# Column halves of the array for attention's and retention's narrow products in a hybrid decoder layer

## The chip, the cores and the metric

The kernel runs on one NeuronCore of a Trainium2 chip. The core's engines are TensorE (PE: matmul, and PEld for its weight loads), VectorE (DVE), ScalarE (ACT), GpSimd (POOL) and SyncE (SP), each with an instruction queue of its own that it works off in order; DMAs are issued from the queues of SP, ACT and POOL. The metric is the device time of one execution in microseconds, as a median over runs; lower is better.

## The reference

One decoder layer over 256 tokens of width 1024, batch 1, all in fp32:

```python
h = rmsnorm(x, mix_norm_g)
rq, rk, rv, rg, mq, mk, mv, ga, gb = split(h @ w_in)
ret = retention(rotary(rq), rotary(rk) * 64 ** -0.5, rv)        # 8 heads, qk 64, v 128, chunks of 128
y_a = (ret * silu(rg)) @ ret_w_branch
att = moba_attention(head_rmsnorm(mq) * 64 ** -0.5, head_rmsnorm(mk), mv, rel_bias)   # 8 heads of 64
y_b = att @ moba_w_branch
x = x + (sigmoid(ga) * y_a + sigmoid(gb) * y_b) @ w_out
x = x + peer(rmsnorm(x, ffn_norm_g), ...)                        # product-key experts, the larger part
```

With 256 tokens there is a single attention block, so attention is causal softmax attention with a bias per head and distance: `softmax(q k^T + bias) v`. Retention works in chunks of 128 tokens:

```python
scores = (q @ k.T) * decay_in            # within a chunk
o_in = scores @ v
kv = (k * k_decay).T @ v                 # state that a chunk leaves behind: 64 x 128 per head
o_cross = (q @ previous_kv) * q_decay
ret = groupnorm(o_in + o_cross)
```

## The kernel before

The sequence is two tiles (`t`) of 128 tokens. The mixer, about the first 250 us, is one stream of projection pieces. A piece is two blocks of 128 rows of a weight matrix by 512 columns. For each piece `i` the main loop (lines 843 to 852) does, in this order: `load_to` issues ring loads on SP's queue; `cut(i + 3)` splits the weights of a piece three ahead into a high and a low part (ACT writes `rhi`, line 147; DVE subtracts and writes `rlo`, line 148); `products(i)` runs the piece's matmuls on PE (lines 230 to 232 or 239 to 241), twelve of 512 columns in the "nat" mode; `early_turns(i)` turns some expert rows for later (DVE line 751; DMAs on ACT's queue, lines 747 and 763); and `pump()` advances each of the first three open generators by one step, up to its next `yield`. The newest epilogue of a projection stands at the front of that list. So attention and retention are generators whose steps are laced between pieces, and the `yield`s set how many pieces lie between two steps. The order of instructions on each engine is the order in which the Python code issues them; nothing is reordered afterwards.

`attention()` does this for each tile: scores into `side` PSUM tiles (line 361, two heads at a time on the row halves of the array), bias (365), maximum (369), exponent on ACT with the row sums into `ssum` (371), then one over the sums into `rs` on DVE (375). After a `yield` it turns the probabilities on PE (383) and evacuates them as `prT` on ACT (384). Two `yield`s later it multiplies: with `prT` as the stationary operand (128 by 128) and 64 columns of `mv` streaming, so that the result `po` has tokens on the partitions and heads in columns (389). DVE multiplies `po` by `rs` into `at` (393), two `yield`s pass, PE turns `at` (400), and `split_to` cuts the turned result into `ah` and `al` for the next projection (401; ACT at line 147, DVE at line 148).

`retention()` begins with the state `kv`: for each pair of heads one product of all 128 columns of `kdec` with the 256 columns of both heads' `rv` (416), evacuated by ACT (418). The result holds the two useful 64 by 128 blocks and two that nobody reads. Line 428 makes the scores on the row halves, line 441 the products with `rv`, and line 446 adds `q @ kv` for the second chunk.

Buffers: `side()` has four PSUM tiles for all short products; the SBUF tag `t2` has four tiles of 128 by 512, shared by the norms (`qn`), the rotary (`ra`, `rb_`, `rqd`), attention's `at` and the gates. Around attention's first tile the rotary of the retention queries runs: for each tile DVE writes `ra` and `rb_` (320, 322), POOL adds them (324), POOL scales one of them into `rqd` (330), and some pumps later PE turns them (273).

Of the kernel before, what the change touches and what calls it, by code (L numbers as in the profile page):

```python
# [18 lines left out]
AF = mybir.ActivationFunctionType  # L19
OP = mybir.AluOpType  # L20
AX = mybir.AxisListType

P = 128
S = 256
# [3 lines left out]
H = 8  # L28
# [47 lines left out]
def layer_kernel(ctx, tc, x, mix_norm_g, w_in, ret_w_branch, moba_q_gain, moba_k_gain, moba_w_branch,  # L76
# [3 lines left out]
    V, A, G, T = nc.vector, nc.scalar, nc.gpsimd, nc.tensor  # L80
# [16 lines left out]
    def side():  # L97
        return psum.tile([P, 512], F32, name="side", bufs=4)
# [46 lines left out]
    def split_to(hi, lo, src, engine=V):  # L145

        A.activation(hi, src, AF.Copy)
        engine.tensor_tensor(lo, src, hi.bitcast(F32), op=OP.subtract)

    def rsqrt_(pool, a, shape, name):  # L150

        y = pool.tile(shape, F32, name=name + "y", bufs=2)
        m = minus_half if len(shape) == 2 else minus_half.rearrange("p (a b) -> p a b", a=shape[1])
        G.tensor_tensor(y, a, m[:, :shape[1]], op=OP.pow)  # L154
        return y
# [17 lines left out]
    ident = cp.tile([P, P], F32, name="ident")  # L173
# [8 lines left out]
    def t4(shape, name, dt=F32):  # L182
        return wk.tile(shape, dt, name=name, tag="t4", bufs=3)

    def t2(shape, name):
        return wk.tile(shape, F32, name=name, tag="t2", bufs=4)
# [90 lines left out]
    mv = ap.tile([P, NT, 512], F32, name="mv", tag="b4a")  # L277
    rqk = [ap.tile([P, 4, S], F32, name=f"rqk{i}", tag="b4" + "fg"[i]) for i in range(2)]
    rqdT = ap.tile([P, 4, P], F32, name="rqdT")
    kdec = ap.tile([P, 512], F32, name="kdec")  # L280
    rv = [ap.tile([P, D], F32, name=f"rv{i}", tag="b4" + "hi"[i]) for i in range(2)]
    kv = ap.tile([P, 4, S], F32, name="kv", tag="b4c")
# [67 lines left out]
    def attention():  # L350
        ssum = wk.tile([P, NT, H], F32, name="ssum")
        for t in range(NT):
            w = (t + 1) * P
            pr = wk.tile([P, H, S], F32, name="pr")
            nh = 512 // w
            for i0 in range(0, 4, nh):
                ps = [side() for _ in range(2)]
                for j in range(nh):
                    for c in range(2):
                        b = slice(c * 64, (c + 1) * 64)  # L360
                        T.matmul(ps[c][:, j * w:(j + 1) * w], mqk[0][b, i0 + j, t * P:(t + 1) * P],
                                 mqk[1][b, i0 + j, :w], start=True, stop=True)
                for c in range(2):
                    n = slice(4 * c + i0, 4 * c + i0 + nh)
                    V.tensor_tensor(pr[:, n, :w], ps[c].rearrange("p (j k) -> p j k", j=nh),
                                    bias[:, n, S - w:], op=OP.add)
                    yield
            sm = wk.tile([P, H], F32, name="smx")
            V.tensor_reduce(sm, pr[:, :, :w], axis=AX.X, op=OP.max, negate=True)
            for h in range(H):  # L370
                A.activation(pr[:, h, :w], pr[:, h, :w], AF.Exp, bias=sm[:, h:h + 1], accum_out=ssum[:, t, h:h + 1])
                if h % 4 == 3:
                    yield
            rs = wk.tile([P, H], F32, name="rs")
            V.reciprocal(rs, ssum[:, t, :])
            yield
            po = side()
            for kt in range(t + 1):
                prT = t4([P, H, P], "prT")
                for q in range(2):  # L380
                    p = side()
                    for j in range(4):
                        T.transpose(p[:, j * P:(j + 1) * P], pr[:, 4 * q + j, kt * P:(kt + 1) * P], ident)
                    A.activation(prT[:, 4 * q:4 * q + 4, :], p.rearrange("p (j i) -> p j i", j=4), AF.Copy)
                yield
                yield
                for i in range(H):
                    h = 2 * (i % 4) + i // 4
                    T.matmul(po[:, h * 64:(h + 1) * 64], prT[:, i, :], mv[:, kt, h * 64:(h + 1) * 64],
                             start=(kt == 0 and i == 0), stop=(kt == t), skip_group_check=True)  # L390
            at = t2([P, 512], "at")
            for c in range(2):
                V.tensor_tensor(at.rearrange("p (i c d) -> p c i d", c=2, d=64)[:, c],
                                po.rearrange("p (i c d) -> p c i d", c=2, d=64)[:, c],
                                rs[:, 4 * c:4 * c + 4, None].to_broadcast([P, 4, 64]), op=OP.mult)
            yield
            yield
            p = side()
            for c in range(4):
                T.transpose(p[:, c * P:(c + 1) * P], at[:, c * P:(c + 1) * P], ident)  # L400
            split_to(ah[0][:, :, t * P:(t + 1) * P], al[0][:, :, t * P:(t + 1) * P],
                     p.rearrange("p (c q) -> p c q", c=4))
            yield

    def mv_epi(o):
# [3 lines left out]
        yield  # L409

    def retention():
        for q in range(2):
            p = side()
            for j in range(2):
                hp = 2 * q + j
                T.matmul(p[:, j * S:(j + 1) * S], kdec[:, hp * P:(hp + 1) * P], rv[0][:, hp * S:(hp + 1) * S],
                         start=True, stop=True)
            A.activation(kv[:, 2 * q:2 * q + 2, :], p.rearrange("p (j e) -> p j e", j=2), AF.Copy)
            yield
        for t in range(NT):  # L420
            s = slice(t * P, (t + 1) * P)

            st = t4([P, H, P], "st")
            ps = [side() for _ in range(2)]
            for j in range(4):
                for c in range(2):
                    b = slice(c * 64, (c + 1) * 64)
                    T.matmul(ps[c][:, j * P:(j + 1) * P], rqk[1][b, j, s], rqk[0][b, j, s], start=True, stop=True)
            for c in range(2):
                V.tensor_tensor(st[:, 4 * c:4 * c + 4, :], ps[c].rearrange("p (j i) -> p j i", j=4),  # L430
                                decay[:, 4 * c:4 * c + 4, :], op=OP.mult)
                yield
            st6 = wk.tile([P, H, 6], F32, name="st6")
            mvv = wk.tile([P, H, 2], F32, name="mvv")
            va = wk.tile([P, H], F32, name="va")
            nm = wk.tile([P, H], F32, name="nm")
            os_ = [side() for _ in range(2)]
            for c in range(2):
                for j in range(4):
                    h = 2 * j + c  # L440
                    T.matmul(os_[c][:, j * P:(j + 1) * P], st[:, 4 * c + j, :], rv[t][:, h * P:(h + 1) * P],
                             start=(j == 0), stop=(t == 0), skip_group_check=True)
            for j in range(4 if t else 0):
                for c in range(2):
                    b = slice(c * 64, (c + 1) * 64)
                    T.matmul(os_[c][:, j * P:(j + 1) * P], rqdT[b, j, :], kv[b, j, c * P:(c + 1) * P], start=False,
                             stop=True, skip_group_check=True)
            for c in range(2):
                for j in range(4):
                    V.bn_stats(st6[:, 4 * c + j, :], os_[c][:, j * P:(j + 1) * P])  # L450
                yield
            for i in range(H):
                V.bn_aggr(mvv[:, i, :], st6[:, i, :])
            V.tensor_scalar(va, mvv[:, :, 1], EPS, None, op0=OP.add)  # L454
            r = rsqrt_(wk, va, [P, H], "gn")
            yield
            V.scalar_tensor_tensor(nm, mvv[:, :, 0], -1.0, r, op0=OP.mult, op1=OP.mult)
            for c in range(2):
                for j in range(4):
                    h, i = 2 * j + c, 4 * c + j  # L460
                    A.activation(ret[:, t, h * P:(h + 1) * P], os_[c][:, j * P:(j + 1) * P], AF.Identity,
                                 bias=nm[:, i:i + 1], scale=r[:, i:i + 1])
                yield
# [153 lines left out]
    def queries(q):  # L617
# [23 lines left out]
        return epi  # L641

    att, rtn, gtd = attention(), retention(), gated()
    w0 = w_in[0]
    hx = (hh, hl)
# [148 lines left out]
    for t in range(NT):  # L794
        for q in range(2):
            c = slice(512 * q, 512 * (q + 1))
# [3 lines left out]
            p = side()  # L800
# [4 lines left out]
    for q in range(2):  # L805
        for t in range(NT):
            n = slice(t * P, (t + 1) * P)
            A.activation(hh[q][:, :, n], sides[2 * t + q], AF.Copy)
    for q in range(2):
        for t in range(NT):  # L810
            n = slice(t * P, (t + 1) * P)
# [460 lines left out]
    for c in range(NK):  # L1272
# [13 lines left out]
        for k in range(KC):  # L1286
            n = c % 2 * NA
            T.matmul(pa[:, n:n + NA], uT[:, k * P:(k + 1) * P], hT[:, k], start=(c % 2 == 0 and k == 0),  # L1288
                     stop=(k == KC - 1), skip_group_check=True)
# [34 lines left out]
    for c in range(NK):  # L1324
# [14 lines left out]
        if c == NK - 5:  # L1339
# [11 lines left out]
            for b in range(KC):  # L1351
                T.matmul(o[b][:, 2 * ND:2 * ND + NXP], gs["accx"][:, b * P:(b + 1) * P], pick, start=False, stop=True,
                         skip_group_check=True)
# [87 lines left out]
```

## Time and profile before

| what | us |
|---|---|
| median of three runs | 943.9 |
| the three runs | 941.56, 943.9, 944.66 |
| the profiled execution, its own time | 942.91 |
| its span, first to last instruction | 941.1 |
| PE busy | 932.6 |
| DVE busy | 794.2 |
| ACT busy | 521.1 |
| POOL busy | 395.0 |

The time of the profiled execution is its span and 1.8 us around it. Busy times of PE are modelled, since matmuls are pipelined: two rows of PE may overlap, and what a product costs is seen from the start of one to the start of the next. In a row of a timeline stand its start, its length, the engine (with a "q" for its instruction sequencer), the line, and output and inputs by name; "x16" means that sixteen records follow each other. In brackets stand the time that the engine was idle before it and what ended that.

### The profile page before, as it was taken

To read this page: it belongs to the slowest core of one execution; us is meant where nothing else is said; L and a number is where in the kernel's file an instruction comes from. 1 tells how busy PE (TensorE), PEld (TensorE's weight loads), DVE (VectorE), ACT (ScalarE), POOL (GpSimd) and SP (SyncE) were. 2 spreads that over 40 slices of the span, in tenths; PEclk is the share of its full clock that TensorE was granted. 3 is DMA by queue.
4 is the path that set the end of the run, shared out by engine and by line. 5 is a ranking of instruction groups with operands and counts; after the bars stand their busy time and mean duration, and the time that the engine had idled before them with its cause. 6 is when DMAs were issued, how large, how long until landed. Compare 5 with 4: busy or idle time off the path is not lost.

```text
span 941.1 us, 19115 instructions
## 1 busy us (share of the span) xinstructions
PE 932.6 (99%) x7192; PEld 894.4 (95%) x7192; DVE 794.2 (84%) x1518; ACT 521.1 (55%) x953; POOL 395.0 (42%) x305
## 2 busy tenths in 40 slices
PE   8999999999999999999999999999999999999998
PEld 6887898998999999999999999999999999999997
DVE  6658557788678999999998999974979989898977
ACT  6554655544644435444687778776454645454553
POOL 3412010000202447534656667763547556464720
PEclk9999999999999999999999999999999999999999
DMA  9899879998799997999999999999999999999993
GB/s 317 236 236 283 241 207 292 306 295 264 244 354 386 406 400 285 402 402 361 375 401 390 382 364 381 380 377 367 370 363 398 409 383 409 383 409 374 409 344 125
DMA packets 110858, 322.50 MB, mean 343 GB/s; under 512 B 11532, under 2 KB 23701, under 8 KB 110638
## 3 DMA queue, kind: packets, MB, share of 16 engines
q1 hardware_dynamic: 64492, 184.43, 55.0%
q0 software_dynamic: 32512, 115.54, 32.5%
q10 hardware_dynamic: 13762, 21.31, 7.6%
q8 instruction: 57, 0.93, 0.4%
q14 instruction: 35, 0.29, 0.1%
HBM read 308.57 MB, written 14.19 MB: 343 GB/s over the span
## 4 chain that ended last, share of the span: by engine, by line
PE 95%; DMA 2%; DVE 1%; ACT 0%; POOL 0%; issue 0%; SPq 0%; DVEq 0%; ACTq 0%; POOLq 0%
PE acc L1288 24%; PE side L737 11%; PE side L1320 9%; PE acc L1320 9%; PE acc L230 6%; PE acc L231 6%; PE acc L232 6%; PE acc L1321 4%; PE side L1321 4%; PE acc L239 3%; PE acc L240 3%; PE acc L241 3%; DMA raw_ring<-in_peer_v_dram 2%; PE side L1318 1%; PE acc L1318 1%; PE acc L1216 1%
## 5 line engine op out<-in xcount | busy, mean ns | idle before, releaser
L1037 POOL DMA_INDIRECT rows<-in_peer_u_dram,eg x86 | 110.5, 1285 | 68.4 <-DVE rows L1048 30.2
L1037 POOL DMA_INDIRECT rows<-in_peer_v_dram,eg x54 | 96.0, 1777 | 73.2 <-DVE vacc L1123 51.2
L737 PE MATMUL side<-ident,raw_ring 128*128 128x128 f32 x768 | 103.0, 277 | 0.0
L737 PEld LDWEIGHTS side<-ident,raw_ring 128*128 128x128 f32 x768 | 93.0, 192 | 0.0
L1165 ACT ACTIVATE oh_buf<-oh_more,tS 128x128 bf16<-128x128 f16 x176 | 58.4, 417 | 0.5 <-DVE oh_more L1160 0.5
L1123 DVE SCALAR_TENSOR_TENSOR vacc<-rows,av,vacc 128x1024 f32<-128x1024 f32 x43 | 55.1, 1282 | 0.1
L1048 DVE SCALAR_TENSOR_TENSOR rows<-rows,h 128x1024 f32<-128x1024 f32 x43 | 53.2, 1249 | 1.4 <-DMA rows<-in_peer_u_dram,eg 1.4
L1260 ACT ACTIVATE cw<-W 128x352 fp32r<-128x352 f32 x58 | 28.7, 495 | 45.3 <-PE acc L1321 43.9
L1261 DVE TENSOR_TENSOR cw<-W,cw 128x352 fp32r<-128x352 f32 x58 | 30.2, 521 | 19.8 <-ACT cw L1260 19.6
L1246 POOL TENSOR_TENSOR W<-W,gl 128x256 f32<-128x256 f32 (+19 forms) x31 | 26.4, 850 | 41.9 <-ACT gl L1245 34.0
L580 POOL DMA_DIRECT2D x1d<-xt x1 | 0.7, 657 | 88.5 <-DVE xt L562 88.5
L1288 PE MATMUL acc<-hTd,raw_ring 128*128 128x128 f32 x288 | 35.1, 276 | 0.0
L1160 DVE TENSOR_TENSOR oh_more<-iota,tI 128x1024 f16<-128x1024 f16 x44 | 34.3, 780 | 0.0
L1161 DVE TENSOR_TENSOR oh_buf<-oh_more,tM 128x1024 f16<-128x1024 f16 x44 | 32.3, 734 | 2.2
L1288 PEld LDWEIGHTS acc<-hTd,raw_ring 128*128 128x128 f32 x288 | 33.6, 192 | 0.0
L154 POOL TENSOR_TENSOR gny<-va,minus_half 128x8 f32<-128x8 f32 x2 | 4.3, 2126 | 67.8 <-DVE va L454 67.8
L1215 PE MATMUL acc<-oh_buf 128*128 128x128 bf16 x176 | 24.4, 220 | 0.0
L1216 PE MATMUL acc<-oh_buf 128*128 128x128 bf16 x176 | 24.4, 219 | 0.0
L1229 ACT ACTIVATE W<-acc 128x512 f32<-128x512 f32 (+20 forms) x44 | 17.2, 391 | 12.0 <-PE acc L1216 10.6
L1248 ACT ACTIVATE W<-acc 128x256 f32<-128x256 f32 (+19 forms) x52 | 18.5, 356 | 4.4 <-PE acc L1288 4.4
L1231 DVE TENSOR_TENSOR W<-acc,W 128x264 f32<-128x264 f32 (+19 forms) x32 | 16.2, 507 | 4.7 <-ACT W L1229 4.5
L1215 PEld LDWEIGHTS <-oh_buf 128*128 128x128 f16 x176 | 19.8, 114 | 0.0
(2695 smaller groups left out, 3484.4 us busy)
## 6 DMA issues: line engine op xcount, KB each, us to landing
raw_ring<-in_peer_v_dram SPq DMA_DIRECT2D x128, 512.0 KB, 8.2
raw_ring<-in_peer_u_dram SPq DMA_DIRECT2D x96, 512.0 KB, 9.9
raw_ring<-in_w_in_dram SPq DMA_DIRECT2D x52, 512.0 KB, 5.5
raw_ring<-turned SPq DMA_DIRECT2D x18, 512.0 KB, 7.1
raw_ring<-in_peer_w_q_dram SPq DMA_DIRECT2D x16, 512.0 KB, 6.1
W<-in_peer_u_dram SPq DMA_DIRECT2D x14, 512.0 KB, 11.0
eraw<-in_peer_u_dram ACTq DMA_DIRECT2D x36, 128.0 KB, 6.5
h<-in_peer_u_dram ACTq DMA_DIRECT2D x36, 128.0 KB, 6.6
```

Of the source, the lines that this page charges most:

```text
L230: T.matmul(o[t], xh[:, s], wh, start=(k == 0), stop=False)
L231: T.matmul(o[t], xh[:, s], wl, start=False, stop=False)
L232: T.matmul(o[t], xl[:, s], wh, start=False, stop=(k == kc - 1))
L737: T.transpose(p[:, k * P:(k + 1) * P], r.rearrange("p (i k) -> p k i", k=KC)[:, 4 * q + k], ident)
L1037: G.indirect_dma_start(out=r, out_offset=None, in_=tab, in_offset=bass.IndirectOffsetOnAxis(ap=eg[:, j:j + 1], axis=0))
L1048: V.scalar_tensor_tensor(r, r, 1.0, h, op0=OP.mult, op1=OP.mult, accum_out=av[:, j:j + 1])
L1123: V.scalar_tensor_tensor(a, r, av[:, j:j + 1], a, op0=OP.mult, op1=OP.add)
L1165: A.activation(o1[:, j], hot[:, 0, :, j], AF.Copy, scale=tS[:, t, k + j:k + j + 1])
L1215: T.matmul(p[:, j * P:(j + 1) * P], hi, o1, start=True, stop=False)
L1288: T.matmul(pa[:, n:n + NA], uT[:, k * P:(k + 1) * P], hT[:, k], start=(c % 2 == 0 and k == 0), stop=(k == KC - 1), skip_group_check=True)
L1320: T.matmul(o[b][:, :2 * ND], vh[:, n], w, start=(c == 0), stop=False, skip_group_check=True)
L1321: T.matmul(o[b][:, :ND], vl[:, n], w[:, :ND], start=False, stop=(c == NK - 1), skip_group_check=True)
```

## The change

Three things change.

Attention's product with `mv` swaps its operands. The 64 columns of `mv` of one head are now the stationary operand, and the 128 columns of `prT` stream. The result comes out turned: 64 rows (the head's dimensions) by 128 tokens. The two heads of a pair write to partitions 0 to 63 and 64 to 127 of the same PSUM tile, which is to say to the two column halves of the array, one after the other in program order.

Since tokens are now in columns, `rs` can no longer be applied per partition. ACT spreads it to `rr` (128 tokens by 512, each head's value 64 times), directly after the reciprocal. After the last product PE turns `rr` into a new `side` tile, ACT copies that to `at`, and DVE multiplies `at` by `po`. The result is already turned, so the four turns of `at` go away; one `yield` is left before `split_to`, where there were two.

Retention's state uses the column halves too: eight products of 64 columns of `kdec` with 128 columns of `rv`, into one `side` tile, with one evacuation in place of two. `kv` holds only the useful blocks, and line 446 reads them at the new place. The number of `yield`s stays.

```diff
             V.reciprocal(rs, ssum[:, t, :])
+            rr = t2([P, 512], "rr")
+            A.activation(rr.rearrange("p (i c d) -> p i c d", c=2, d=64),
+                         rs.rearrange("p (c i) -> p i c", c=2)[:, :, :, None].to_broadcast([P, 4, 2, 64]), AF.Copy)
             yield
             po = side()
             for kt in range(t + 1):
...
-                for i in range(H):
-                    h = 2 * (i % 4) + i // 4
-                    T.matmul(po[:, h * 64:(h + 1) * 64], prT[:, i, :], mv[:, kt, h * 64:(h + 1) * 64],
-                             start=(kt == 0 and i == 0), stop=(kt == t), skip_group_check=True)
+                for i in range(4):
+                    for c in range(2):
+                        h = 2 * i + c
+                        T.matmul(po[c * 64:(c + 1) * 64, i * P:(i + 1) * P], mv[:, kt, h * 64:(h + 1) * 64],
+                                 prT[:, 4 * c + i, :], start=(kt == 0 and i == 0), stop=(kt == t), skip_group_check=True)
+            p = side()
+            for i in range(4):
+                T.transpose(p[:, i * P:(i + 1) * P], rr[:, i * P:(i + 1) * P], ident)
             at = t2([P, 512], "at")
-            for c in range(2):
-                V.tensor_tensor(at.rearrange("p (i c d) -> p c i d", c=2, d=64)[:, c],
-                                po.rearrange("p (i c d) -> p c i d", c=2, d=64)[:, c],
-                                rs[:, 4 * c:4 * c + 4, None].to_broadcast([P, 4, 64]), op=OP.mult)
-            yield
-            yield
-            p = side()
-            for c in range(4):
-                T.transpose(p[:, c * P:(c + 1) * P], at[:, c * P:(c + 1) * P], ident)
+            A.activation(at, p, AF.Copy)
+            V.tensor_tensor(at, at, po, op=OP.mult)
+            yield
             split_to(ah[0][:, :, t * P:(t + 1) * P], al[0][:, :, t * P:(t + 1) * P],
-                     p.rearrange("p (c q) -> p c q", c=4))
+                     at.rearrange("p (c q) -> p c q", c=4))
             yield
...
-        for q in range(2):
-            p = side()
-            for j in range(2):
-                hp = 2 * q + j
-                T.matmul(p[:, j * S:(j + 1) * S], kdec[:, hp * P:(hp + 1) * P], rv[0][:, hp * S:(hp + 1) * S],
-                         start=True, stop=True)
-            A.activation(kv[:, 2 * q:2 * q + 2, :], p.rearrange("p (j e) -> p j e", j=2), AF.Copy)
-            yield
+        p = side()
+        for j in range(4):
+            for c in range(2):
+                n = j * P + c * 64
+                T.matmul(p[c * 64:(c + 1) * 64, j * P:(j + 1) * P], kdec[:, n:n + 64], rv[0][:, 2 * n:2 * n + P],
+                         start=(j == 0), stop=True, skip_group_check=True)
+        A.activation(kv[:, :, :P], p.rearrange("p (j e) -> p j e", j=4), AF.Copy)
+        yield
+        yield
...
-                    T.matmul(os_[c][:, j * P:(j + 1) * P], rqdT[b, j, :], kv[b, j, c * P:(c + 1) * P], start=False,
+                    T.matmul(os_[c][:, j * P:(j + 1) * P], rqdT[b, j, :], kv[b, j, :P], start=False,
                              stop=True, skip_group_check=True)
```

## The prediction

> **What bounds the kernel now.** I read the engines' busy shares first, then the chain of work that ended last, then the waits of PE.
>
> ```profile
> PE 932.6 (99%) x7192; PEld 894.4 (95%) x7192; DVE 794.2 (84%) x1518; ACT 521.1 (55%) x953; POOL 395.0 (42%) x305
> ...
> PE 95%; DMA 2%; DVE 1%; ACT 0%; POOL 0%; issue 0%; SPq 0%; DVEq 0%; ACTq 0%; POOLq 0%
> ...
> PE side L780 <- DVE ident L769: 1.5, 1, 1.5
> PE side L1320 <- DVE cw L1261: 1.1, 2, 0.6
> ```
>
> PE is the bound: it makes 95% of the chain, and its two largest named waits are 1.5 us at the very start and 1.1 us near 700 us. So nearly every microsecond put on or taken off PE's stream moves the end, while a wait of DVE, ACT or POOL is free until PE meets it. The table of windows says the same of the stretch that the change touches:
>
> ```profile
> 50.00:100.00 50.00, 50.00 (x250) 40.91 (x249) 37.14 (x47) 25.06 (x51) 9.78 (x6) 1.00 0.97 268
> 100.00:150.00 50.00, 50.00 (x341) 44.47 (x340) 30.63 (x59) 27.31 (x44) 2.61 (x1) 1.00 0.79 227
> ```
>
> PE is busy in all of these 100 us, at the full granted clock (1.00). Busy time is modelled, so I price PE by the steps from start to start in its timeline.
>
> **The products, before.** Each fp32 product is two records ("passes"): 24 products of line 389 give 48.
>
> ```profile
> L389 PE MATMUL side<-mv,prT x48: 217/275/276, 68.3 to 123.3; 128*128 128x64 f32 x48
> L416 PE MATMUL side<-rv,kdec x8: 377/380/382, 99.5 to 104.6; 128*128 128x256 f32 x8
> ```
>
> The first group of line 389 (t = 0) lies between two pieces of the projection:
>
> ```profile
> 67.36 0.39 PE L231 MATMUL acc<-rlo__601,hh 128*128 128x512 f32 x1
> 67.59 0.39 PE L232 MATMUL acc<-rhi__600,hl 128*128 128x512 f32 x1
> 67.82 0.60 PE L273 MATMUL side<-ident,ra 128*128 128x128 f32 x4
> 68.26 1.90 PE L389 MATMUL side<-mv,prT 128*128 128x64 f32 x16
> 69.96 0.48 PE L230 MATMUL acc<-rhi__634,hh 128*128 128x512 f32 x1
> 70.28 0.39 PE L231 MATMUL acc<-rlo__635,hh 128*128 128x512 f32 x1
> ```
>
> A projection product follows the last after 0.23 us (67.36 to 67.59). L231 starts at 70.28, so L230 would have stood at 70.05 undisturbed: the 16 passes cost 70.05 - 68.26 = 1.79 us, 0.112 a pass. Line 416, counted in the same way:
>
> ```profile
> 99.48 1.02 PE L416 MATMUL side<-rv,kdec 128*128 128x256 f32 x4
> 100.15 0.58 PE L230 MATMUL acc<-rhi__908,hh 128*128 128x512 f32 x1
> 100.57 0.40 PE L231 MATMUL acc<-rlo__909,hh 128*128 128x512 f32 x1
> ```
>
> 100.57 - 0.23 - 99.48 = 0.86 for four passes, 0.215 a pass and 1.72 for both groups. Together the changed products cost 3 x 1.79 + 1.72 = 7.1 us.
>
> **The products, after.** No row shows column halves. The nearest is line 428, which uses row halves: two products of 64 rows, one after the other in program order, 16 passes of 128 columns.
>
> ```profile
> 107.17 0.39 PE L231 MATMUL acc<-rlo__933,hh 128*128 128x512 f32 x1
> 107.40 0.39 PE L232 MATMUL acc<-rhi__932,hl 128*128 128x512 f32 x1
> 107.72 1.16 PE L428 MATMUL side<-rqk,rqk 64*128 64x128 f32 x16
> 108.81 0.50 PE L230 MATMUL acc<-rhi__958,hh 128*128 128x512 f32 x1
> 109.15 0.39 PE L231 MATMUL acc<-rlo__959,hh 128*128 128x512 f32 x1
> ```
>
> Without the group L428 the next product would have started at 107.63; after it L230 stands in effect at 108.92. The group costs 1.29 us: eight pairs at 0.112 are 0.90, and 0.39 goes into and out of the half mode (0.09 before its first start). The new groups are of that size: three of line 389 and one of line 416 (now 16 passes of 128 columns). Bounds for a pass: not below 0.054, since 256 streamed columns took 0.215 and a pair shares a stream of 128; not above 0.112, a full pass. I take line 428's 0.056, the row nearest in shape. Then each attention group saves 1.79 - 1.29 = 0.50, the state product 1.72 - 1.29 = 0.43, together **-1.9 us**.
>
> The Trainium skill, TensorEngine Tiling (Array Packing), section Key Properties, speaks against the change: switching the tiling mode drains the engine. It gives no figure; line 428's 0.39 would be that drain and agrees. Were it nothing, the sum would be 4 x 0.39 = 1.6 us better.
>
> The turning products stay eight single passes (of `rr`, not of `at`): nothing. They move up behind the products, and need only `rr`, long written by then, and a free PSUM tile.
>
> **The new wait.** Until now nobody but DVE needed `rs`. Now ACT copies it into `rr`, in the queue where ACT also cuts the weights and evacuates `prT`, which the products read. For t = 0 these queues read:
>
> ```profile
> 62.05 1.04 ACT L147 ACTIVATE rhi__600<-raw_ring 128x1024 fp32r<-128x1024 f32 x1
> 62.99 1.04 ACT L147 ACTIVATE rhi__634<-raw_ring 128x1024 fp32r<-128x1024 f32 x1
> 66.26 0.36 ACTq L763 DMA_DIRECT2D turned<-eT  x1
> 66.67 0.60 ACT L384 ACTIVATE prT<-side 128x512 f32<-128x512 f32 x1 [2.63 <-DVE eT L751]
> 67.16 0.59 ACT L384 ACTIVATE prT<-side 128x512 f32<-128x512 f32 x1
> ...
> 66.73 0.74 DVE L322 TENSOR_TENSOR rb__624<-acc,rope 128x256 f32<-128x256 f32 x2
> 67.39 0.18 DVE L375 RECIPROCAL rs<-ssum 128x8 f32<-128x8 f32 x1
> 67.49 1.17 DVE L148 TENSOR_TENSOR rlo__635<-raw_ring,rhi__634 128x1024 fp32r<-128x1024 f32 x1
> ...
> 65.77 1.29 POOL L324 TENSOR_TENSOR ra<-ra,rb__617 128x512 f32<-128x512 f32 x1 [22.73 <-DVE rb__617 L322]
> 67.61 2.18 POOL L324 TENSOR_TENSOR ra<-ra,rb__624 128x512 f32<-128x512 f32 x1 [0.55 <-DVE rs L375]
> ```
>
> DVE runs the reciprocal as the last work of its pump, just ahead of the next cut's `rlo__635`. So on ACT `rr` stands between `rhi__600` and `rhi__634`, and it can't start before 67.57, when the reciprocal ends. A second condition is its buffer. The tag `t2` has four; there the rotary holds `ra` and `rb_` of both tiles. Only the two `rb_` come free, `rqd` takes one and `rr` the other. If they are given in the order of release, `rr` gets the second, read last by POOL's addition that starts at 67.61. That took 2.18 beside `rlo__635`; in the changed kernel `rlo__635` is itself late, so I give it the first one's 1.29: free at 68.90.
>
> From there by ACT's own steps: `rr` 68.95; `rhi__634` 0.49 later (the step between the two `prT`), 69.44; `prT` 0.94 later (`rhi__600` to `rhi__634`), 70.38; the second `prT` 70.87, done 71.47. The DMA of L763 is issued meanwhile. PE can begin the group at 71.5, where it was ready at 68.26. From its first start a half-mode group takes 108.92 - 107.72 = 1.20, so PE leaves at 72.7 instead of 70.05: **+2.65 us**, for t = 0, with its own gain already in it. For the rest, two attention groups and the state product give -1.43. **Sum +1.2 us.**
>
> Behind `rr` wait: `rhi__634` and with it DVE's `rlo__635` (done near 71.7; PE asks for it near 73.4, after the four turns), the store of `eT` and four loads of `eraw`, which nobody needs for some pumps (they feed DVE's next turn, some ten us on), and the following cuts, of which PE takes one per 12 x 0.23 = 2.8 us, itself 2.65 later now. I count them as nothing; if that cover fails, PE stalls again by the part of a microsecond that is missing. SP's ring loads start later by as much as the cuts do, and four pieces ahead. ACT's `at` copy (about 0.6) waits for PE's turns; behind it stands a cut two pieces away from its use.
>
> For t = 1 the same chain has slack:
>
> ```profile
> 102.19 1.06 ACT L467 ACTIVATE rv<-acc 128x512 f32<-128x512 f32 x2
> 103.14 0.58 ACT L418 ACTIVATE kv<-side 128x512 f32<-128x512 f32 x1
> 104.09 0.16 DVE L375 RECIPROCAL rs<-ssum 128x8 f32<-128x8 f32 x1
> 111.67 1.89 PE L389 MATMUL side<-mv,prT 128*128 128x64 f32 x16
> ```
>
> ACT would wait for 104.25, about 1 us, and PE starts the products only at 111.67; no rotary holds buffers then. Attention also ends a pump sooner per tile (one `yield` less), which shifts t = 1 against the projection, with microseconds to spare. ACT's and DVE's other changes (one evacuation less, two more copies, one multiply for two) lie beside PE.
>
> **The rivals.**
> - *The other buffer.* If `rr` gets the first `rb_`, only the reciprocal binds: all of t = 0 is 68.95 - 67.62 = 1.33 earlier, sum -0.1.
> - *No wait.* If `rr` finds both early enough, the whole gain stays: -1.9. Against it: the reciprocal's row stands behind a full DVE queue, and ACT's `prT` stood 0.5 us ahead of the products as it was.
> - *The halves don't overlap* (the change doesn't do what it says): both column halves take their operand from the same 128 rows, which row halves don't. At 0.112 a pass each group costs 1.79 + 0.39 = 2.18. For t = 0 PE leaves at 71.5 + 2.09 = 73.6 (+3.55), the other groups add 2 x 0.39 + 0.46: +4.8, slower. With 64 passes it decides from about 0.08 us a pass on (1.2 + 64 x 0.025 = 2.8). Against it: line 428 pairs.
> - *The clock falls in the stall.* The first 16 passes of the kernel ran at half pace ((3.63 - 0.42) / 15 = 0.21 a pass, against 0.112):
>
> ```profile
> 1.47 3.63 PE L780 MATMUL side<-ident 128*128 128x128 f32 x16 [1.47 <-DVE ident L769]
> L780 PE MATMUL side<-ident 128*128 128x128 f32 x16 | 3.6, 419 | 1.5 <-DVE ident L769 1.5
> ```
>
> If 3.2 us of idle PE brought that back for as long as those rows last, half of 3.4 us more is lost: +2.9. No wait in the middle of this trace is long enough to tell. The Trainium skill, TensorE: Matmul & The Clock Gate, Part 1, has such a rule, with an idle window of about 3.4 us; the wait would fall just short of it.
>
> **How the numbers follow.** The sum is made on the profiled execution, 942.9 us; the median of the three runs is 943.9, inside their spread of 3.1. I put the sum on the median: 945.1. Chances: forecast 0.42 (945.1), other buffer 0.20 (943.8), no wait 0.12 (942.0), no overlap 0.17 (948.7), clock 0.04 (946.8), anything else 0.05. The range goes from the no-wait case less half a microsecond to the no-overlap case: 941.5 to 948.7. A measurement here tells about 0.3% (2.8 us) from no change. Faster by that needs the no-wait case and luck: 0.07. Slower comes from most of no overlap, half of the clock case and the edge of the forecast: 0.23. Same: 0.70.
>
> **What would show it.** In the changed trace: pairs of passes of the new products starting within some ns, 16 in about 1.2 us (else no overlap); one PE wait of about 3 us near 68 us with ACT's `prT` as releaser, and `rr` on ACT released by POOL (forecast) or by DVE's reciprocal (other buffer); no such wait near 110; granted clock 1.00 between 70 and 80. The forecast is wrong if PE meets other waits, such as a late cut, or a PSUM tile that the turns of `rr` wait for.

## The result and the profile after

| | us |
|---|---|
| kernel before, median of six runs | 943.61 (941.56 to 944.66) |
| changed kernel, median of six runs | 951.61 (948.43 to 952.96) |
| ratio, 95% interval | 1.0088 [1.0072, 1.0104] |
| profiled execution of the changed kernel, its own time | 950.12, span 948.4 |

The change makes the kernel slower by 8.0 us. The forecast was 945.1 with a range of 941.5 to 948.7, so the time lies outside, on the slow side.

The page of the changed kernel, engines' busy shares:

```profile
PE 935.3 (99%) x7200; PEld 894.3 (94%) x7200; DVE 795.6 (84%) x1516; ACT 523.0 (55%) x956; POOL 393.4 (41%) x305
```

PE's busy time rose by only 2.7 us, while the span rose by 7.3. The rest of the time is waiting, and the waits of PE name it (total, times, longest, in us):

```profile
PE side L417 <- ACT rv L469: 4.1, 1, 4.1
PE side L393 <- ACT prT L387: 2.0, 1, 2.0
```

The second is the wait that was forecast. The first, twice as long, was not in the forecast at all. The next longest, 1.5 us for `ident` at the very start, stood in the kernel before as well. Here is the first place, attention's products for t = 0, in the timeline:

```profile
66.95 0.18 DVE L375 RECIPROCAL rs<-ssum 128x8 f32<-128x8 f32 x1
...
67.17 1.28 POOL L324 TENSOR_TENSOR ra<-ra,rb__624 128x512 f32<-128x512 f32 x1 [0.55 <-DVE rs L375]
...
68.04 0.60 PE L273 MATMUL side<-ident,ra 128*128 128x128 f32 x4
68.48 0.63 ACT L377 ACTIVATE rr<-rs 128x512 f32<-128x512 f32 x1 [5.83 <-POOL ra L324]
...
69.02 1.04 ACT L147 ACTIVATE rhi__636<-raw_ring 128x1024 fp32r<-128x1024 f32 x1
...
70.44 0.59 ACT L387 ACTIVATE prT<-side 128x512 f32<-128x512 f32 x1
...
70.59 1.60 PE L393 MATMUL side<-prT,mv 128*64 128x128 f32 x16 [1.96 <-ACT prT L387]
...
71.08 0.85 PEld L393 LDWEIGHTS side<-prT,mv 128*64 128x64 f32 x14 [0.30 <-ACT prT L387]
...
72.13 1.12 PE L397 MATMUL side<-ident,rr 128*128 128x128 f32 x4
```

The order is the one forecast: `rr` is released by POOL's addition (L324), the cut and the two `prT` follow on ACT, and PE's products (L393) wait for `prT`. The heads of one pair now need both `prT` tiles, so after the first two passes PE's weight loads (PEld) wait again, until 71.03, when the second `prT` ends. The group takes 72.13 - 70.59 = 1.54 here.

The second place is retention's state, and beyond it an attention group with no wait:

```profile
104.28 1.04 ACT L147 ACTIVATE rhi__938<-raw_ring 128x1024 fp32r<-128x1024 f32 x1
...
104.69 0.66 PE L417 MATMUL side<-rv,kdec 128*64 128x128 f32 x8
...
107.12 0.16 DVE L375 RECIPROCAL rs<-ssum 128x8 f32<-128x8 f32 x1
107.38 0.63 ACT L377 ACTIVATE rr<-rs 128x512 f32<-128x512 f32 x1 [2.06 <-DVE rs L375]
107.92 1.04 ACT L147 ACTIVATE rhi__964<-raw_ring 128x1024 fp32r<-128x1024 f32 x1
108.86 1.06 ACT L469 ACTIVATE rv<-acc 128x512 f32<-128x512 f32 x2
...
109.49 1.09 PE L417 MATMUL side<-rv,kdec 128*64 128x128 f32 x8 [4.14 <-ACT rv L469]
...
117.03 0.39 PE L232 MATMUL acc<-rhi__938,hl 128*128 128x512 f32 x1
...
117.35 1.09 PE L393 MATMUL side<-prT,mv 128*64 128x128 f32 x16
...
118.37 1.09 PE L386 MATMUL side<-ident,pr 128*128 128x128 f32 x8
```

Eight passes of the state product run at 104.69, and the other eight only at 109.49. They read the second half of `rv`, whose evacuation (L469) stands on ACT behind three others: the cut `rhi__938`, `rr`, which waited 2.06 us for DVE's reciprocal, and the cut `rhi__964`. In the kernel before, `rv` (102.19) ran ahead of the reciprocal (104.09). Now attention has one `yield` less per tile, so for t = 1 the reciprocal and `rr` are issued a pump earlier, ahead of that last cut and of `rv`. The last three rows price the column halves in the way in which the prediction priced line 389: a product 0.23 after L232 would have stood at 117.26, L386 starts at 118.37, so 16 passes in column halves cost 1.11 us, against 1.79.

The third thing is in the table of windows (stretch; its length; busy time of PE, PEld, DVE, ACT and POOL with instruction counts; granted clock; DMA share; GB/s):

```profile
70.60:73.00 2.40, 2.34 (x21) 1.91 (x21) 1.71 (x2) 2.40 (x4) 0.00 (x0) 0.79 1.02 236
73.00:75.50 2.50, 2.50 (x8) 2.01 (x7) 2.50 (x4) 1.84 (x3) 0.00 (x0) 0.52 0.84 248
...
109.50:113.20 3.70, 3.70 (x15) 2.87 (x16) 2.17 (x3) 2.83 (x5) 0.00 (x0) 0.54 0.39 84
113.20:118.00 4.80, 4.80 (x31) 3.77 (x31) 2.24 (x3) 1.06 (x1) 0.00 (x0) 1.00 1.00 329
```

After each of the two waits the granted clock falls to about one half. In the timeline projection products follow each other at 0.43 us instead of 0.23 from 72.01 to 75.42 and from 109.56 to 112.97, each time for 3.41 us. At half pace 3.41 us cost 1.7 (1.6 by the step from 0.43 to 0.23), twice 3.2 to 3.4.

Together this is the whole loss. The mixer (from the projection product that starts at 62.60 before and at 62.81 after, to the last L231, at 240.05 and 248.82) takes 177.45 us before and 186.01 after, 8.56 more. The rows give: waits 2.0 at the first place, 0.5 inside that group (1.54 against 1.02 without a wait, at 117.35) and 4.1 at the second; half clock 3.2 to 3.4; the halves' own gain, three times 1.79 - 1.11 and once 1.72 - 1.22 (measured in the last experiment), -2.5; and two smaller losses, 0.7 (turns, L386 at 103.11 to L417 at 104.69, 1.58 against 0.88) and 0.3 (scores), described with the last experiment. The sum is 8.3 to 8.5. From the expert phase to the end the changed kernel regains 1.7 us: from the first product that reads `cw` to the last product it takes 286.70 us instead of 288.44, and the waits of L1320 for `cw` that the kernel before had are gone from the list.

### The profile page after: what moved, and what is told of

Its sections match the earlier page's. It is cut to its first block, busy times and chain, and to the rows that moved or that the text cites. A ratio compares the mean times of both kernels' runs of the same rounds, so it can differ in the third digit from the quotient of the medians.

```text
span 948.4 us, 19132 instructions
## 1 busy us (share of the span) xinstructions
PE 935.3 (99%) x7200; PEld 894.3 (94%) x7200; DVE 795.6 (84%) x1516; ACT 523.0 (55%) x956; POOL 393.4 (41%) x305
## 4 chain that ended last, share of the span: by engine, by line
PE 92%; DVE 2%; ACT 2%; issue 1%; POOL 1%; DMA 1%; ACTq 0%; DVEq 0%; POOLq 0%
PE acc L1290 24%; PE side L739 11%; PE acc L1322 9%; PE side L1322 9%; PE acc L230 4%; PE acc L231 4%; PE acc L232 4%; PE acc L1323 4%; PE side L1323 4%; PE acc L240 3%; PE acc L239 3%; PE acc L241 3%; PE side L1320 2%; PE acc L1320 2%; PE acc L1217 1%
## 5 line engine op out<-in xcount | busy, mean ns | idle before, releaser
L1039 POOL DMA_INDIRECT rows<-in_peer_v_dram,eg x54 | 98.0, 1814 | 73.6 <-DVE vacc L1125 57.1
```

Source lines behind the costliest of these rows:

```text
L1039: G.indirect_dma_start(out=r, out_offset=None, in_=tab, in_offset=bass.IndirectOffsetOnAxis(ap=eg[:, j:j + 1], axis=0))
```

## Experiments

Three questions were open: which part of the change costs how much; whether the half clock comes from the waits; and whether the waits can be taken away with the column halves kept. The theory was that the halves gain some 2 us, that `rr`'s place on ACT and the state product's single group make the waits, and that the half clock follows a wait. The main rival was that the halves themselves, or the extra copies on ACT, cost time wherever they stand. Diffs are against the changed kernel unless said otherwise. Four kernels ran beside 27 runs of the kernel before (median 943.45), the other four beside 34 (942.96).

| kernel | median, us | ratio, 95% interval |
|---|---|---|
| attention's part alone | 947.82 | 1.0043 [1.0028, 1.0058] |
| retention's part alone | 946.43 | 1.0031 [1.0018, 1.0044] |
| `rr` late, state in two groups | 943.12 | 0.9999 [0.9985, 1.0013] |
| waits filled with useless turns | 949.74 | 1.0059 [1.0038, 1.0081] |
| `rr` early, state in two groups | 947.48 | 1.0044 [1.0032, 1.0057] |
| the same, `rr` in a buffer of its own | 944.72 | 1.0014 [1.0000, 1.0027] |
| `rr` late in its own buffer, two groups | 942.45 | 0.9992 [0.9976, 1.0007] |
| `rr` late in its own buffer, one group a pump later | 941.62 | 0.9993 [0.9978, 1.0009] |

### Each part alone

Attention's part alone keeps the state product as it was before:

```diff
     def retention():
-        p = side()
-        for j in range(4):
-            for c in range(2):
...
+        for q in range(2):
+            p = side()
+            for j in range(2):
+                hp = 2 * q + j
+                T.matmul(p[:, j * S:(j + 1) * S], kdec[:, hp * P:(hp + 1) * P], rv[0][:, hp * S:(hp + 1) * S],
+                         start=True, stop=True)
+            A.activation(kv[:, 2 * q:2 * q + 2, :], p.rearrange("p (j e) -> p j e", j=2), AF.Copy)
+            yield
...
```

> Attention's part of the change alone; retention's state as before. Theory (waits and clock): the changed kernel lost time in two PE waits (2.1 us at attention's first tile for prT behind rr, 4.3 us in the state product for rv) and in the 3.4 us of half clock that followed each (1.7 us each), and the column halves do save 0.5 us a group. Here then: one PE wait of about 2 us near 70 us, one stretch of half clock behind it, no wait near 105; +2.1 + 1.7 - 1.5 = +2.3 us, about 946. Rival (the halves themselves cost: three of the four groups are here): about three quarters of the +8, near +6, with groups longer than 1.3 us.

It took 4.4 us more than the kernel before. PE's waits, and the windows behind the first of them:

```profile
PE side L393 <- ACT prT L387: 2.6, 1, 2.6
...
PE side L417 <- ACT rv L468: 1.1, 1, 1.1
```

```profile
71.00:77.70 6.70, 6.37 (x28) 5.17 (x29) 6.01 (x7) 4.69 (x7) 0.00 (x0) 0.50 0.99 277
```

The granted clock was 0.50 for 6.8 us, two stretches of 3.41. This is the slowest of its ten runs, though; only three of them show a mean clock of 0.998 or less, and the four at 1.00 took 946.4 to 948.0, so most of the 4.4 us is there without the half clock. The second wait is telling: here the second half of the state product runs a pump later, as before, and still waits 1.1 us for `rv`. `rr` of t = 1 stands ahead of it on ACT, so its price may be paid by retention; the kernels with `rr` late, below, test that.

Retention's part alone is the last two pieces of the change on the kernel before, so there is no `rr`:

```diff
     def retention():
-        for q in range(2):
-            p = side()
...
-            yield
+        p = side()
+        for j in range(4):
+            for c in range(2):
+                n = j * P + c * 64
...
+        yield
+        yield
...
```

> Retention's part alone; attention as before. Theory: the second half of the state product now stands one pump earlier than the evacuation of the second half of rv needs. In the kernel before, the product stood at 99.5 us and that evacuation ended at 103.2: a PE wait of 3.5 to 4 us near 100 us, half clock behind it (1.7 us), 0.4 us saved: about +5 us, 948.5. Rival (the wait in the changed kernel came only from rr, which held up ACT): no wait here, -0.4 us. Rival (the halves themselves cost): about a quarter of +8, +2.

It took 3.0 us more. The wait is there without any `rr`:

```profile
102.61 0.66 PE L416 MATMUL side<-rv,kdec 128*64 128x128 f32 x8
...
104.28 1.04 ACT L147 ACTIVATE rhi__958<-raw_ring 128x1024 fp32r<-128x1024 f32 x1
105.23 1.06 ACT L468 ACTIVATE rv<-acc 128x512 f32<-128x512 f32 x2
...
105.85 0.66 PE L416 MATMUL side<-rv,kdec 128*64 128x128 f32 x8 [2.58 <-ACT rv L468]
```

The second eight passes wait 2.6 us for `rv` behind one cut. In the changed kernel the same wait was 4.1. The difference of 1.5 is not what `rr` costs, since there attention's turns come a pump earlier and keep PE busy for 1.6 us just ahead of the state product. In the changed kernel's own rows ACT waits for `rr` and copies it from 105.32, the end of the cut, to 107.92; without these 2.6 us the wait of 4.1 would by these rows have been 1.5 (an estimate). In this profiled execution the granted clock stayed at 1.00 behind the wait (the same columns as above):

```profile
106.00:110.00 4.00, 4.00 (x27) 3.28 (x26) 2.51 (x4) 1.90 (x4) 0.00 (x0) 1.00 0.70 190
```

The clocks of its twelve runs lie between 0.996 and 1.00. Seven of them are at 0.998 or less, and none of the 61 runs of the kernel before. The profiled one is at 0.998, but it lost its clock elsewhere: for 3.41 us from 12.59 on, at the very start of the mixer, behind a wait of 1.5 us for the low part of the first weights, where the kernel before waited 0.2:

```profile
PE acc L231 <- POOL rlo__205 L148: 1.5, 1, 1.5
```

So a mean clock below 1 doesn't say where the clock fell. The two parts together, 4.4 + 3.0 = 7.4, make nearly the whole 8.0 by the medians, in which the half clock has different shares.

### Waits filled with work

PE runs 18 useless turns ahead of attention's products for t = 0 and 36 ahead of the state product, so that it isn't idle while it has to wait. They write into the PSUM tile that the products then overwrite.

```diff
+                for i in range(0 if t else 18):
+                    T.transpose(po[:, :P], ident, ident)
                 for i in range(4):
                     for c in range(2):
...
         p = side()
+        for i in range(36):
+            T.transpose(p[:, :P], ident, ident)
         for j in range(4):
```

> The changed kernel with useless turns of the identity on PE ahead of the two products that wait: 18 (about 2.0 us at 0.109) ahead of attention's first products, 36 (about 3.9 us) ahead of the state product. PE works as long as it waited; nothing else changes. Theory (an idle PE of some 2 us brings the half clock): no stretch of half clock in the mixer, 2 x 1.7 = 3.4 us faster than the changed kernel, about 948 (+4.6 on the kernel before). Rival (the clock fell for another reason, or its fall costs nothing): as the changed kernel, about 951.6, or slower by up to 1 us.

PE has 54 more products and the kernel is not slower than the changed one: the median is 1.9 us lower, and the ratio 1.0059 against 1.0088, some 2.7 us, with intervals that overlap. The profiled mixer is 2.5 us shorter (183.54 against 186.01). The time alone would not settle it; the clock does. The stretches in which the clock had been half:

```profile
71.00:76.00 5.00, 4.84 (x34) 3.86 (x35) 4.31 (x5) 4.36 (x7) 0.00 (x0) 1.00 0.95 263
...
109.00:115.00 6.00, 6.00 (x33) 4.70 (x30) 3.78 (x5) 3.38 (x5) 0.00 (x0) 1.00 0.79 223
```

The clock is 1.00 there, and in all six runs of this kernel its mean is 0.999 or 1.00; the six runs of the changed kernel show 0.993 to 0.998. One stretch of 3.41 us at one half takes 3.41 x 0.5 / 948 = 0.0018 off the mean, so those six had about one to four of them. With the idle time filled the half clock is gone, with the column halves all in place: it comes from PE's waits. Less was gained than expected: in this execution `rr` started 1.10 us after L273 (69.00 against 67.90), where it was 0.44 in the changed kernel's profile (68.48 against 68.04), so that part of a microsecond was lost on other grounds, and PE still waited 0.6 for `prT`.

### `rr` early or late, state in one or two groups

The third kernel of the first four moves `rr` behind the last `prT`, in the same `t2` buffer, and splits the state product into two groups, a pump apart:

```diff
-            rr = t2([P, 512], "rr")
-            A.activation(rr.rearrange("p (i c d) -> p i c d", c=2, d=64),
-                         rs.rearrange("p (c i) -> p i c", c=2)[:, :, :, None].to_broadcast([P, 4, 2, 64]), AF.Copy)
             yield
             po = side()
...
                     A.activation(prT[:, 4 * q:4 * q + 4, :], p.rearrange("p (j i) -> p j i", j=4), AF.Copy)
+                if kt == t:
+                    rr = t2([P, 512], "rr")
+                    A.activation(...)
                 yield
...
+        for q in range(2):
+            p = side()
+            for j in range(2):
+                for c in range(2):
+                    n = (2 * q + j) * P + c * 64
+                    T.matmul(p[c * 64:(c + 1) * 64, j * P:(j + 1) * P], kdec[:, n:n + 64], rv[0][:, 2 * n:2 * n + P], ...)
+            A.activation(kv[:, 2 * q:2 * q + 2, :P], p[:, :2 * P].rearrange("p (j e) -> p j e", j=2), AF.Copy)
+            yield
```

> Both parts, with both suspected waits taken away: rr is written after prT of the last step instead of ahead of it, and the state product is again two groups (of 8 passes on the column halves) a pump apart. Theory: no PE wait over 0.5 us in the mixer, granted clock 1.00 throughout, three attention groups at 1.29 instead of 1.79 us, the state about even (0.84 against 0.86 a group): -1.5 us, about 942. Rival (the halves cost): slower than before by several us, still.

It is level with the kernel before; the gain of 1.5 us that was expected lies at the very edge of its interval. One wait was left, of the turns of `rr` (L398):

```profile
67.51 2.18 POOL L324 TENSOR_TENSOR ra<-ra,rb__624 128x512 f32<-128x512 f32 x1 [0.55 <-DVE rs L375]
...
69.72 0.63 ACT L387 ACTIVATE rr<-rs 128x512 f32<-128x512 f32 x1 [2.07 <-POOL ra L324]
...
70.40 0.66 PE L398 MATMUL side<-ident,rr 128*128 128x128 f32 x4 [0.65 <-ACT rr L387]
```

The products (L394) no longer wait, but `rr` still does: POOL's addition now runs beside DVE's work and takes 2.18 us instead of 1.28, and only when it ends at 69.69 is the buffer free. The order and the buffer had to be told apart. So `rr` goes back to its early place, with the state in two groups, once in `t2` and once in a tile of its own:

```diff
-            rr = t2([P, 512], "rr")
+            rr = wk.tile([P, 512], F32, name="rrs")
```

> The changed kernel with only the state product put back into two groups a pump apart (on the column halves); rr stays where the change put it. Theory: the wait of 2 us at attention's first tile stays, with half clock behind it in most executions; the wait for rv goes: +2.1 + up to 1.7 - 1.5, about +2 (945.5). Rival (rr's delay of ACT also reaches the second group): a wait of about 1 us at the second group, +3.

> As the run before, but rr has an SBUF tile of its own instead of one of the four of t2. It need not wait for POOL's second addition of the rotary, only for the reciprocal, which ends 1.35 us sooner. Theory: rr released by DVE's reciprocal, the PE wait at attention's first tile falls from 2.1 to about 0.8 us, too short for the half clock: +0.8 - 1.5, about -0.7 (942.8). Rival (the buffer doesn't bind): as the run before.

With the state in two groups and `rr` in `t2` the kernel took 4.5 us more than the kernel before, as attention's part alone did. PE's waits:

```profile
PE side L393 <- ACT prT L387: 2.6, 1, 2.6
...
PE side L418 <- ACT rv L469: 1.2, 1, 1.2
```

The clock fell here too, for 3.41 us. With a buffer of its own `rr` starts right behind the reciprocal, not behind POOL:

```profile
68.33 0.18 DVE L375 RECIPROCAL rs<-ssum 128x8 f32<-128x8 f32 x1
...
68.55 0.63 ACT L377 ACTIVATE rrs<-rs 128x512 f32<-128x512 f32 x1 [4.52 <-DVE rs L375]
68.56 1.28 POOL L324 TENSOR_TENSOR ra<-ra,rb__624 128x512 f32<-128x512 f32 x1 [0.55 <-DVE rs L375]
...
70.66 1.57 PE L393 MATMUL side<-prT,mv 128*64 128x128 f32 x16 [1.30 <-ACT prT L387]
```

This takes 2.8 us off (947.48 to 944.72). The wait for `prT` is 1.3 instead of 2.6, so the buffer is worth 1.3 us of wait; and the clock holds, in this profile and with a mean of 0.999 or 1.00 in all ten runs:

```profile
70.70:75.00 4.30, 4.25 (x31) 3.43 (x32) 4.26 (x5) 4.21 (x6) 0.25 (x1) 1.00 0.96 253
```

Its two waits of 1.3 and 1.1 us brought no half clock. What is left against the kernel before is `rr`'s place on ACT, ahead of what PE waits for.

The last two kernels have `rr` late and in its own tile, one with the state in two groups, one with a single group that begins a pump later (so with all of `rv` evacuated):

```diff
     def retention():
+        yield
         p = side()
...
         A.activation(kv[:, :, :P], p.rearrange("p (j e) -> p j e", j=4), AF.Copy)
         yield
-        yield
```

> rr written behind prT of the last step, into a tile of its own; the state product in two groups on the column halves. In the run with the late rr in t2, PE waited 0.65 us for rr, which waited for POOL's addition. Theory: that wait goes; no wait over 0.3 us is left, three groups save 0.5 us: -1.5 us on the kernel before, in the mixer as in the median (942).

> As the run before, with the state product as one group of the column halves, a pump later than in the changed kernel, when both halves of rv have been evacuated. Theory: no PE wait at it; 0.4 us better than two groups, -1.9 us on the kernel before (941.5). Rival (ACT evacuates rv too late for that pump as well): a wait of a microsecond or more near 105 us.

Both medians are the lowest of the study, 942.45 and 941.62, and neither can be told from the kernel before by its interval. Between 50 and 245 us PE's longest wait is 0.2 in both. With `rr` late and two groups the wait of 1.1 for `rv` is gone, so there it was `rr` that delayed it; and the rival falls, since the halves and the copies on ACT, placed so, cost no time that can be measured. Two of the twelve runs of the last kernel, its slowest (945.30 and 945.82), show mean clocks of 0.998 and 0.997; where theirs fell is not on record. The last kernel, in the timeline of the state product and of the scores behind it:

```profile
102.28 1.05 ACT L470 ACTIVATE rv<-acc 128x512 f32<-128x512 f32 x2
...
103.23 0.39 PE L232 MATMUL acc<-rhi__916,hl 128*128 128x512 f32 x1
...
103.55 1.09 PE L419 MATMUL side<-rv,kdec 128*64 128x128 f32 x16
...
104.58 0.50 PE L230 MATMUL acc<-rhi__938,hh 128*128 128x512 f32 x1
...
104.91 0.40 PE L231 MATMUL acc<-rlo__939,hh 128*128 128x512 f32 x1
...
108.55 1.09 PE L383 MATMUL side<-ident,pr 128*128 128x128 f32 x8
...
109.57 1.48 PE L431 MATMUL side<-rqk,rqk 64*128 64x128 f32 x16
...
110.97 0.50 PE L230 MATMUL acc<-rhi__962,hh 128*128 128x512 f32 x1
```

`rv` is done at 103.33, and the 16 passes follow without a wait: 104.91 - 0.23 - (103.23 + 0.23) = 1.22 us, against 1.72 in two groups before. Its mixer takes 176.04 us, 1.41 less than before. By the groups it should be 2.5 less. The rows say where the rest went. Retention's scores (L431) now follow turns and not a projection product, and take 110.97 - 109.57 = 1.40 to the next projection product, where the same 16 passes took 108.81 - 107.72 = 1.09 before: 0.3. Attention's second tile runs a pump earlier, and its turns (L383, from 99.10 on) run while ACT is still at the exponents that they read: counted like the other groups they cost 1.60 us, and 0.88 before: 0.7. That gives -1.5. Why the scores take longer there was not tried.

And little of the 1.41 reaches the end. At the first product that reads `cw` PE is 1.06 ahead of the kernel before (647.81 against 648.87; 0.35 was lost at the start, ahead of the change), at the last product 0.44 (936.87 against 937.31). The expert phase waits for what is no part of the change, here in the same kernel's timeline:

```profile
690.62 1.06 ACT L147 ACTIVATE rhi__7884<-raw_ring 128x1024 fp32r<-128x1024 f32 x1 [2.89 <-DMA raw_ring<-in_peer_v_dram]
...
691.71 1.23 DVE L148 TENSOR_TENSOR rlo__7885<-raw_ring,rhi__7884 128x1024 fp32r<-128x1024 f32 x1 [2.72 <-ACT rhi__7884 L147]
...
692.85 0.52 DVE L1264 TENSOR_TENSOR cw<-W,cw 128x352 fp32r<-128x352 f32 x1
...
693.42 0.43 PE L1323 MATMUL side<-cw,rhi__7884 128*128 128x352 f32 x1 [1.38 <-DVE cw L1264]
```

The cut on ACT waits 2.89 us for its weights from memory, DVE's `cw` stands behind that cut's `rlo`, and PE waits 1.4 for `cw`. In the kernel before PE waited 0.6 at this place; from the first product with `cw` to the end it took 288.44 us, and here 289.06: PE comes earlier, the weights hardly do. That the loads give the gain back is read from the two profiles; no run tested it.

## Why the prediction was wrong, point by point

- **The halves pair: right.** The pairs overlap, the rival against it is out. A group without waits costs 1.11 (attention) and 1.22 (state) where 1.29 was taken from the row halves; the gain would be 2.5 instead of 1.9. The Trainium skill, TensorEngine Tiling (Array Packing), section Key Properties, says that a change of mode drains the engine. Eight pairs at 0.112 are 0.90, so about 0.2 to 0.3 of each group goes into and out of the half mode, less than the 0.39 of the row halves.
- **The new wait for t = 0: right in every link, somewhat too long.** Buffer of the second `rb_`, POOL's addition at 1.28 (forecast 1.29), `rr`, cut, two `prT`. From the start of L273 to the end of the group (start of L397) the changed kernel takes 72.13 - 68.04 = 4.09, where the forecast was 72.7 - 67.82 = 4.88. The term of +2.65 was +1.9. DVE's reciprocal was 0.44 earlier (66.95 against 67.39) and PE 0.22 later, and no row of the kernel before told that. Other profiles have the wait 0.6 longer, nearer to the forecast. The rival of the other buffer priced the difference between POOL's addition and the reciprocal at 1.33; it measured 1.3 with the buffer of its own.
- **The state product: this step failed.** It was priced as a gain of 0.43, from its passes alone, with the remark that the number of `yield`s stays. The number stays, but what happens in each step does not: all of the product now runs in the first pump, and half of it reads the second half of `rv`. The code issues that evacuation just ahead of the first pump, but ACT comes to it 2.7 us after PE has reached the product, behind exponents and a cut; one pump later it was done. The rows that say so stand in the prediction: `rv` evacuated from 102.19 on, between products at 99.48 and 103.99. The first of the two copies is the one needed, and PE follows 0.62 after its start (105.23 to 105.85 with retention's part alone): 102.8. PE, ready for the second half at about 99.9, would wait 2.9 us. With retention's part alone it waited 2.6.
- **`rr` for t = 1: "the same chain has slack" was wrong too.** The slack was looked for at the products of line 389, the copy's own user. Behind the waiting copy on ACT stood a cut and the evacuation of `rv`, whose user is retention. This made 1.1 us of wait even with two state groups, and by its rows 2.6 of the 4.1 with one. The prediction named what is queued behind `rr` for t = 0, but not for t = 1. It took the removed `yield` as a shift "with microseconds to spare"; that shift put `rr` ahead of `rv`, where in the rows of the kernel before `rv` runs first.
- **The clock in the stall: a rival with a chance of 0.04, and it came true twice.** It was held unlikely because 3.2 us of idle PE would fall just short of the window. The mechanism was priced well (1.7 a time); the threshold was taken from the Trainium skill and not from a row. The Trainium skill, TensorE: Matmul & The Clock Gate, Part 1, speaks of an idle window of about 3.4 us, free-running: the lengths of the half clock, 3.41 us or twice that, agree with such a window, but 2.2 us between the starts of two products was enough here, with PE idle for 2.0 of it; the last section has the rows.
- **The sum.** Forecast +2.65 - 1.43 = +1.2. The change cost 8.0: about +1.9 at t = 0 and -1.9 for the other groups' gain, the terms that were forecast, then +4.1 for the state's wait, +3.2 to +3.4 for the clock, +1.0 for the two small losses, which makes 8.3 to 8.5 in the mixer, less what the expert phase gives back. With the two waits gone but the halves kept, the kernel can't be told from the kernel before (0.9993, interval 0.9978 to 1.0009). The forecast took a gain in the mixer to move the end by as much, which was also too simple: of 1.41 us in the last kernel's mixer 0.44 is left at its last product.

## What to carry to other kernels

When two steps of a generator are merged, ask for each operand when the engine that writes it gets there; neither an unchanged number of steps nor the order in the code says that. When an operation is put on an engine's in-order queue, list what is queued behind it at every place where it runs, and look for the user of each of those, not of the operation alone; do the same when a `yield` goes, since it moves every later step. Put a helper copy behind the work that the bound engine waits for, in a buffer that nothing slow holds; and if PE must idle for nearly two microseconds, price the risk of a stretch of half clock with it.

## What was not expected of the hardware

**Half clock after short idles.** Gaps between the starts of two PE products, and what followed in the profiled executions: 2.23 and 4.42 us (changed kernel), 3.41 us of half clock each; 2.86 (attention's part alone), 6.83; 2.86 (`rr` early, two groups), 3.41; 1.96 at the very start (retention's part alone), 3.41, and 2.86 later in the same execution, none; 1.57 and 1.53 (own buffer), none, and no sign of any in the ten runs' means. So the gap's length alone does not decide. It begins late: in the changed kernel the wait ended at 70.59 and the clock fell at 72.01.

The traces suggest why. The half clock between two products always lasts 3.41 us or twice that, and in the changed kernel the end of the first stretch (75.42) and the start of the second (109.56) lie ten times 3.41 us apart, as if the clock were set anew every 3.41 us. If the edges of an execution's own half-clock stretch are continued in such steps, PE's idle time in a window (3.41 less its busy time) sorts the cases:

| profiled execution | window, us | PE idle in it, us | clock in the next window |
|---|---|---|---|
| changed kernel | 106.15 to 109.56 | 3.3 | half |
| attention's part alone | 67.41 to 70.83 | 2.1 | half |
| changed kernel | 68.60 to 72.01 | 2.0 | half |
| `rr` early, two groups | 69.66 to 73.08 | 1.8 | half |
| retention's part alone | 9.18 to 12.59 | 1.8 | half |
| retention's part alone | 101.34 to 104.75 | 1.5 | full |
| `rr` early, two groups | 107.21 to 110.62 | 1.2 | full |
| retention's part alone | 104.75 to 108.16 | 1.1 | full |

By these rows 1.8 us of idle time in one window is enough and 1.5 is not; the wait of 2.6 in retention's part alone was spared since an edge (104.75) cut it in two. This is read from a few windows, and no run moved a wait against the edges to test it. One thing doesn't fit: with attention's part alone a second stretch followed a window in which PE idled for only 0.5.

Two kernels that idle for about as long can thus differ by 1.7 us or a multiple, and so can two executions of one kernel: the changed kernel's run with a mean clock of 0.998 took 948.43, the two with 0.993 took 952.27 and 952.96.

**Row halves behind turns.** The same 16 passes of the scores took 1.40 us behind a group of turns and 1.09 behind a projection product, in the changed kernel (119.39 to 120.80) as in the last one shown. The cause stays open.
